# A decoder layer's opening: the conditioning vector spread by split fp32r products, half of the first input row block loaded from a second queue, weight casts before row copies

## The chip, the cores and the metric

The kernel runs on one core of a Trainium2 chip. The metric is device time in microseconds (us), from the first to the last work of the program on that core. The kernel before has a median of 720.72 us over 3 runs (719.94 to 721.26).

## The reference, cut to what matters

One layer of a decoder trunk, for 1024 tokens of 1024 channels, in float32:

```python
c_act = jax.nn.silu(c)
mod = c_act @ mod_w + mod_b                       # 1024 -> 3 x 1024
shift, scale, gate = jnp.split(mod, 3, axis=-1)
h = rmsnorm(x, norm_g) * (1.0 + scale) + shift
u = h @ w_in                                      # 1024 -> 5120
cv, cg, cs, lx, ls = split(u)
v = layernorm(causal_depthwise_conv(cv * sigmoid(cg), dw_w, dw_b))     # 31 taps
y_conv = (silu(v) @ pw2_w + pw2_b) * silu(cs)
xs = causal_depthwise_conv(lx, sc_w, sc_b)                              # 4 taps
r, i = sigmoid(xs @ wr + br), sigmoid(xs @ wi + bi)                     # block diagonal
hs = linear_scan(a(r), b(r, i, xs))
y_lru = hs * silu(ls)
x = x + (1.0 + gate) * (concat(y_conv, y_lru) @ w_out)
return rmsnorm(x, final_g)
```

## The kernel before

Channels lie on the 128 partitions, tokens along the free axis, so `x` is eight tiles `x0` to `x7` of 128x1024, and `T` = 1024, `H` = 512, `KT` = 8. Every large product is made in fp32r with the operands split in two: for an activation `u` and a weight `w`, `hi` is the value rounded to fp32r, `lo` the remainder, and three products `hi*hi`, `lo*hi`, `hi*lo` of 512 columns are added up in PSUM. ScalarE writes `hi` (a cast, a copy or a scaled activation), VectorE, GpSimd or an accumulating DMA makes `lo`.

All work is handed to a planner, class `Plan`. `S.op(engine, cost, emit, prio, reads, writes, ...)` records one step. `Plan.order` then plays the kernel forward with the costs written down and lets each engine take, of the steps that are ready, the one with the smallest priority; `Plan.run` emits the instructions in the order found. The order on each engine is therefore fixed when the kernel is built, and every engine works strictly through its own list. A table, `TURNS`, keyed by engine, first and last buffer of a step and a count, adds small amounts to priorities. `SP` stands for the queue from which nearly all loads are issued; loads accumulating in DRAM or SBUF are issued from GpSimd (`POOL`), stores of the last stage partly from ScalarE (`ACT`).

The opening, which sets when the first product of `w_in` can begin:

- `V` is a small table of all vectors, `c` among them, loaded first (L1483). SP's next loads are in the order of `LOADS`: `s0` (the first block of the transposed modulation matrix that gives `scale`, called `modw`), `w0` (weights of the first four output tiles for channel block 0, called `fraw`), `a0` and `b0` (the two halves of `x0`, 256 KB each), then `s1 w1 x1 s2 W2 x2` and so on.
- ScalarE makes `cs = silu(c)` as a 128x8 tile (L1834). `spread_c` (L1843) turns it into a row that lies on all partitions, `c_row`: for each of the 8 channel blocks a matmul whose stationary operand is one column of `cs`, repeated 128 times, and whose moving operand is the identity, in plain fp32. One such fp32 matmul is two instructions in the trace. Four blocks go into each of two PSUM tiles, `z` = 0 and 1.
- `first_dot` (L1938) multiplies `modw` by `c_row` on VectorE straight out of PSUM, in two halves, each with a sum along the row (L1434), and ScalarE copies `c_row` to SBUF as `sc`, at priority -101. The later blocks (`dot`, L1929) read `sc`. From the sums comes `gs`, one number per channel (L1961).
- `uh0`, the scaled `x0` rounded, comes from VectorE for the first half (L1456). `fhi` and `flo` are the split of `fraw`, `ul` the remainder of `uh`. `fw_mm` (L1884) then multiplies: 21 matmuls of 512 columns for each of the 8 channel blocks into the tiles called `first`.
- To keep TensorE at work meanwhile, 12 matmuls of a 128x128 tile of ones by itself, `idle_mm` (L1841, two instructions each, written into `token_stats`), stand in its list: 4 before the spread, 8 behind it (`IDLE`, `IDLE0`).

```python
cs, ps_c = ctile("cs", KT), [mm_tile(f"c_row{z}") for z in (0, 1)]
ACT(-130, lambda: cs, lambda: V[:, OFF["c"]:OFF["c"] + KT], AF.Silu, KT, w=[("cs", 0)])
def spread_c(z):
    for k in range(4 * z, 4 * z + 4):
        pe.matmul(half(ps_c[z], 0)()[:, k % 4 * P:k % 4 * P + P], cs[:, k:k + 1].to_broadcast([P, P]), ident,
                  start=True, stop=True)
```

After the opening come, in the order of the string `ORDER`, the other tiles of `u`: `iN` is output tile N of `w_in` (L1575, matmuls into `ps`), `gN` the two gate products of recurrence head N (`gates`, L2315, which read `xsh` and `xsl`, the split of `xs`), `iM+iN` two tiles done together with fewer products (`duo`, into `up` and `dn`; VectorE and GpSimd make the sums). Then come the recurrent half of `w_out` (`lru_pair`, `lx`, `lw`, `lc`; `lru_sums` makes the sums of activations it needs at a priority that holds `LTP`), `pw2`, and the other half of `w_out` with the last norm.

Of the kernel before, what the change touches and what calls it, by code (L numbers as in the profile page):

```python
# [9 lines left out]
F32 = mybir.dt.float32  # L10
F32R = mybir.dt.float32r
# [23 lines left out]
ORDER = "i10 i24 i2 g0 i25 i11 i3 i26 i33 i12 i4 g1 i34 i23 g2 i13 i35 i5 i27 g3 i20 i39 i14 i6 i28+i36 i15 i30+i37 i7 i29+i38 g6 g4 g5 i31 i19 i22+i18 g7 i21"  # L35
# [65 lines left out]
DENG = {14: ("POOL", "DMA", "DVE"), 17: ("POOL", "DVE", "DVE"), 20: ("DVE", "DVE", "DMA"), 21: ("DMA", "DMA", "DVE"), 24: ("DMA", "DVE", "POOL"), 26: ("DVE", "DMA", "DMA"), 27: ("POOL", "DMA", "POOL"), 30: ("DVE", "DVE", "DVE"), 35: ("DMA", "POOL", "DVE"), 36: ("POOL", "POOL", "POOL"), 39: ("DVE", "DVE", "POOL"), 40: ("DVE", "DVE", "DMA")}  # L101
# [7 lines left out]
LTP = 0.0  # L109
# [68 lines left out]
PDIRECT = (4,)  # L178
# [25 lines left out]
    ("ACT", "c1", "cq1_13", 0): -2.2,  # L204
# [39 lines left out]
    ("ACT", "cr4", "cr4", 0): 7.9,  # L244
    ("ACT", "cr4", "vha2", 0): 6.4,
# [43 lines left out]
    ("ACT", "r7", "r7", 0): -1.2,  # L289
    ("ACT", "r7", "r7", 1): -3.2,  # L290
# [73 lines left out]
    ("ACT", "vt1", "vhc1", 0): -0.1,  # L364
# [4 lines left out]
    ("ACT", "whi32", "wlo32", 0): -0.1,  # L369
    ("ACT", "whipw20", "wlopw20", 0): -2,  # L370
# [35 lines left out]
    ("DVE", "acc0", "lp0", 1): -0.3,  # L406
# [13 lines left out]
    ("DVE", "c2", "caccs2", 11): -0.1,  # L420
# [15 lines left out]
    ("DVE", "c4", "caccs4", 13): -0.2,  # L436
# [21 lines left out]
    ("DVE", "c6", "cacc6", 0): -0.6,  # L458
    ("DVE", "c6", "caccs6", 2): 1,
    ("DVE", "c6", "caccs6", 4): -0.5,  # L460
    ("DVE", "c6", "caccs6", 6): 2,
    ("DVE", "c6", "caccs6", 7): 0.2,
    ("DVE", "c6", "caccs6", 8): -0.3,
    ("DVE", "c6", "caccs6", 9): 1.6,
    ("DVE", "c6", "caccs6", 10): -2.4,
    ("DVE", "c6", "caccs6", 11): 1.5,
    ("DVE", "c6", "caccs6", 13): 1.4,
    ("DVE", "c6", "caccs6", 14): 2.6,
    ("DVE", "c6", "lnwide", 0): -0.3,
    ("DVE", "c6", "mean", 0): 0.3,  # L470
    ("DVE", "c6", "vla3", 0): -0.1,
    ("DVE", "c6", "vu3", 0): 2.7,
# [15 lines left out]
    ("DVE", "c7", "caccs7", 15): -0.1,  # L488
# [5 lines left out]
    ("DVE", "c7", "vt3", 1): -0.5,  # L494
    ("DVE", "cr0", "lnwide", 0): 3,
# [3 lines left out]
    ("DVE", "cr1", "vt0", 0): -1,  # L499
# [4 lines left out]
    ("DVE", "cr4", "mean", 0): 1.4,  # L504
    ("DVE", "csum", "c7", 0): -1,
# [4 lines left out]
    ("DVE", "fin0", "zout_0", 0): -2.7,  # L510
    ("DVE", "fraw0", "flo0", 0): 0.1,
# [28 lines left out]
    ("DVE", "rawout0_0", "rawout0_1", 1): -2,  # L540
# [9 lines left out]
    ("DVE", "rawpw21_1", "rawpw21_0", 0): -4,  # L550
# [6 lines left out]
    ("DVE", "sls3", "r3", 0): -0.1,  # L557
# [6 lines left out]
    ("DVE", "up33", "xs5", 0): -1,  # L564
    ("DVE", "up33", "xs5", 2): -0.2,
# [4 lines left out]
    ("DVE", "v0", "cacc0", 12): -0.3,  # L570
    ("DVE", "v0", "caccs0", 0): -0.2,
# [13 lines left out]
    ("DVE", "v2", "caccs2", 8): 0.2,  # L585
# [785 lines left out]
def hymba_layer(ctx: ExitStack, tc: tile.TileContext, xT, vecs, mod_w, w_first, w_in,  # L1371
# [229 lines left out]
    def half(b, i):  # L1601
        return part(b, i * H, i * H + H)
# [237 lines left out]
    def idle_mm():  # L1840
        pe.matmul(psb()[:, :P], ones, ones, start=True, stop=True)  # L1841
# [1244 lines left out]
```

## Time and profile before

| | |
|---|---|
| median of the runs | 720.72 us |
| profiled execution, its own time | 722.46 us |
| span of its instructions | 720.6 us |
| TensorE busy | 710.4 us (99%), 3230 matmuls |
| VectorE busy | 641.5 us (89%) |
| ScalarE busy | 477.3 us (66%) |
| GpSimd busy | 218.2 us (30%) |
| mean granted TensorE clock | 0.997 |

The page divides the span into busy time by engine; a matmul's record lasts until its result is written, so records of neighbouring matmuls overlap, and the time from one start to the next is what a matmul costs in a stream. The chain of work that ended last is followed back from the last instruction, at each step to what released it. A load is shown as the instruction that issues it and with the time from that issue to its landing.

### The profile page before, as it was taken

The numbers are of one execution on the slowest core, as the hardware profiler recorded it, in microseconds if no ns is written. First come the engines' busy times: TensorE is split into PE (matmuls) and PEld (weight loads), VectorE is DVE, ScalarE is ACT, GpSimd is POOL, SyncE is SP. The second block draws the span as 40 slices with busy tenths as digits, with TensorE's granted clock in tenths as the row PEclk, the third lists the DMA queues.
The fourth block names the chain that finished last, engine by engine and source line by source line (L and its number), as shares of the span: only waits on it lengthen the run. The fifth ranks groups of instructions, "written<-read, shape, count | busy, mean of one in ns | idle before, by whom it ended". The sixth has DMA issues, their size and how long they took to land.

```text
span 720.6 us, 9035 instructions
## 1 busy us (share of the span) xinstructions
PE 710.4 (99%) x3230; PEld 590.3 (82%) x3230; DVE 641.5 (89%) x885; ACT 477.3 (66%) x604; POOL 218.2 (30%) x188
## 2 busy tenths in 40 slices
PE   9999999999999999999999999999999999999995
PEld 8888888888888888888888888887887888878885
DVE  7989999799999989969988998998589976998747
ACT  7651598847857874974794979937589653744422
POOL 0022434543676752474162351100102100100001
PEclk9999999999999999999999999999999999999998
DMA  9935458999697999699664339999638755892006
GB/s 341 407 154 176 73 149 204 246 270 204 119 253 187 250 240 229 169 230 206 211 176 117 88 98 282 264 301 246 161 81 204 183 124 123 239 279 93 27 1 233
DMA packets 45500, 137.53 MB, mean 191 GB/s; under 512 B 5144, under 2 KB 14624, under 8 KB 45344
## 3 DMA queue, kind: packets, MB, share of 16 engines
q0 software_dynamic: 16848, 45.52, 35.2%
q1 hardware_dynamic: 27600, 90.53, 35.1%
q10 hardware_dynamic: 1008, 0.92, 0.4%
q8 instruction: 25, 0.41, 0.2%
q14 instruction: 19, 0.16, 0.1%
HBM read 84.22 MB, written 25.69 MB: 153 GB/s over the span
## 4 chain that ended last, share of the span: by engine, by line
PE 78%; DVE 10%; ACT 4%; issue 4%; DMA 3%; POOL 1%; DVEq 0%; POOLq 0%; ACTq 0%
PE ps L1575 34%; PE xpw L1751 6%; PE xout L1751 6%; PE first L1884 5%; PE dn L2713 3%; PE ypw L1751 3%; PE gate L2315 3%; PE dn L1575 3%; DVE caccs L1434 2%; PE up L1575 2%; PE lx L2468 2%; PE y L1721 1%; DMA wlo<-in_w_out_dram 1%; DMA wloout<-in_w_out_dram 1%; PE zpw L1751 1%
## 5 line engine op out<-in xcount | busy, mean ns | idle before, releaser
L1575 PE MATMUL ps<-uh,whi 128*128 128x512 f32 x448 | 138.0, 389 | 0.0
L1575 PE MATMUL ps<-uh,wlo 128*128 128x512 f32 x448 | 137.9, 389 | 0.0
L1575 PE MATMUL ps<-ul,whi 128*128 128x512 f32 x448 | 137.9, 389 | 0.0
L1575 PEld LDWEIGHTS ps<-uh,wlo 128*128 128x128 f32 x448 | 84.1, 188 | 17.5
L1575 PEld LDWEIGHTS ps<-ul,whi 128*128 128x128 f32 x448 | 84.1, 188 | 17.4
L1575 PEld LDWEIGHTS ps<-uh,whi 128*128 128x128 f32 x448 | 84.0, 188 | 17.4
L1434 DVE SCALAR_TENSOR_TENSOR cacc<-v,V,cacc 128x511 f32<-128x511 f32 (+14 forms) x90 | 66.5, 739 | 0.3
L1434 DVE SCALAR_TENSOR_TENSOR caccs<-v,V,caccs 128x511 f32<-128x511 f32 (+6 forms) x84 | 62.4, 743 | 1.0
L1434 DVE SCALAR_TENSOR_TENSOR caccs<-c,wsum,caccs 128x511 f32<-128x511 f32 (+6 forms) x84 | 62.2, 740 | 0.8
L1415 ACT CAST whi<-raw 128x1024 fp32r<-128x1024 f32 (+1 forms) x44 | 44.1, 1006 | 26.7 <-issue 14.0
L1423 ACT ACT_TABLE_LOAD x46 | 59.0, 1283 | 3.2 <-DVE r L2327 1.1
L1442 POOL TENSOR_TENSOR wlo<-raw,whi 128x1024 fp32r<-128x1024 f32 (+1 forms) x15 | 36.4, 2428 | 75.5 <-ACT whi L1415 73.5
L1447 POOL DMA_DIRECT2D es<-cq x30 | 28.3, 943 | 32.1 <-DMA es<-cq 11.1
L1434 DVE SCALAR_TENSOR_TENSOR modw<-modw,sc 128x1024 f32<-128x1024 f32 x23 | 32.7, 1425 | 0.0
L1442 DVE TENSOR_TENSOR wlo<-raw,whi 128x1024 fp32r<-128x1024 f32 (+1 forms) x22 | 30.7, 1395 | 0.6 <-ACT whi L1415 0.6
L1447 POOL DMA_DIRECT2D oo<-co x26 | 26.5, 1054 | 11.1 <-issue 5.5
L1423 ACT ACTIVATE uh<-x,shift 128x512 fp32r<-128x512 f32 x16 | 10.5, 713 | 23.9 <-PE ps L1575 23.9
L1442 POOL TENSOR_TENSOR o<-fin,bc 128x256 f32<-128x256 f32 (+1 forms) x6 | 4.9, 831 | 70.8 <-ACT bc L1415 70.8
L1447 POOL DMA_DIRECT2D accd<-acc x8 | 7.3, 914 | 62.1 <-ACT acc L1423 44.2
L1423 ACT ACTIVATE finsq<-fin 128x512 f32<-128x512 f32 (+2 forms) x14 | 7.9, 570 | 27.0 <-DVE fin L1434 15.1
L1423 ACT ACTIVATE cq<-v,V 128x511 f32<-128x511 f32 (+14 forms) x30 | 21.0, 707 | 6.5 <-DVE r L2327 3.1
L1447 POOL DMA_DIRECT2D lz<-in_w_out_dram x16 | 14.4, 987 | 34.4 <-ACT lz L1423 30.5
(525 smaller groups left out, 1937.8 us busy)
## 6 DMA issues: line engine op xcount, KB each, us to landing
raw<-in_w_in_dram SPq DMA_DIRECT2D x36, 512.0 KB, 4.6
modw<-in_mod_w_dram SPq DMA_DIRECT2D x24, 512.0 KB, 7.6
scsd<-scs SPq DMA_DIRECT2D x8, 512.0 KB, 3.9
raw<-in_w_out_dram SPq DMA_DIRECT2D x8, 512.0 KB, 4.5
accd<-acc POOLq DMA_DIRECT2D x8, 512.0 KB, 8.0
rawpw<-in_pw_dram SPq DMA_DIRECT2D x8, 512.0 KB, 3.9
scsr<-scsd SPq DMA_DIRECT2D x8, 512.0 KB, 4.3
rawout<-in_w_out_dram SPq DMA_DIRECT2D x8, 512.0 KB, 4.4
```

The costliest lines, as they stand in the source:

```text
L1415: act.copy(out(), in_())
L1423: act.activation(out=out(), in_=in_(), func=func, **kw)
L1434: dve.scalar_tensor_tensor(out=out(), in0=in0(), scalar=scalar, in1=in1(), op0=op0, op1=op1, accum_out=accum)
L1442: lambda: e.tensor_tensor(out=out(), in0=a(), in1=b(), op=op), prio, r, w,
L1447: return S.op("POOL", ISSUE, lambda: pool.dma_start(out(), a(), accum_op=ALU.add), prio, r, w, lag=RATE * n / T, after=after, flight=flight)
L1575: pe.matmul(ps()[:, a - off:b - off], k3(lhs)()[:, at, :], rhs[k]()[:, a:b], start=(k == first and lhs is wh and rhs is xh and (a - off) % ...
L1721: pe.matmul(to(), half(*lhs)()[:, j * P:j * P + P], half(*rhs)()[:, c0:c1], start=a == "S1" and j == 0 and t == 0, stop=j == KT // 2 - 1 a ...
L1751: pe.matmul(half(ps, 0)(), half(*lhs)()[:, j * P:j * P + P], half(*rhs)(), start=start and at == 0 and i == 0, stop=at == len(order) - 1 a ...
L1884: pe.matmul(ps()[:, a - off:b - off], fw_part(lhs, k, i * P, i * P + P)(), rhs()[:, a:b], start=k == 0 and lhs is wh and rhs is xh, stop=k ...
L2315: pe.matmul(ps()[:, c0:c1], lhs()[:, j, :], rhs()[:, c0:c1], start=st == 0, stop=st == 2)
L2468: pe.matmul(half(ps, h)(), lhs()[:, o:o + P], half(*rhs)(), start=begin and at == 0 and t == 0, stop=at == len(order) - 1 and t == len(ter ...
L2713: pe.matmul(half(ps, h)(), lhs()[:, o:o + P], half(rhs, z)(), start=begin and j == 0 and t == 0, stop=j == NJ - 1 and t == 2, skip_group_c ...
```

## The change

`silu(c)` is computed twice on ScalarE, once rounded to fp32r (`cs_hi`) and once in fp32 (`cs`); VectorE makes the remainder `cs_lo`. Instead of 8 fp32 matmuls by the identity, 16 fp32r matmuls are made, 8 with `cs_hi` and 8 with `cs_lo`, adding up in the same PSUM tiles. The identity is written as fp32r and read as fp32 elsewhere. The idle matmuls read one column of ones, repeated on both sides, instead of a 128x128 tile. The first half of `x0` is issued from ScalarE's queue as ScalarE's first step; SP no longer issues it. The copies of `c_row` to `sc` get priority -98.9 instead of -101, which is behind the cast of the first weights (-99). Beyond the opening, the gates of heads 4, 5, 6 and the pair of tiles 18 and 22 change their order in `ORDER`, `LTP` becomes -0.5, and some 135 lines of `TURNS` are added, removed or altered, nearly all in steps far behind the opening.

```diff
-ORDER = "... i29+i38 g6 g4 g5 i31 i19 i22+i18 g7 i21"
+ORDER = "... i29+i38 g4 g5 g6 i31 i19 i18+i22 g7 i21"
...
-DENG = {14: ("POOL", "DMA", "DVE"), ...}
+DENG = {14: ("POOL", "DMA", "DVE"), ..., 34: ("DVE", "DVE", "DVE"), ...}
...
-LTP = 0.0
+LTP = -0.5
...
-XADDP = -1.5
+XADDP = 0.3
 TSRC = "POOL"
 HSP = -60
+CSR, XQ, SCP = True, "ACT", -98.9
...
-CENG = {..., 22: "POOL", ...}
+CENG = {..., 22: "DVE", ..., 37: "POOL", 40: "DVE"}
...
-PDIRECT = (4,)
+PDIRECT = ()
...
-    ("ACT", "cr4", "cr4", 0): 7.9,
-    ("ACT", "cr4", "vha2", 0): 6.4,
+    ("ACT", "cr4", "cr4", 0): 7.6,
+    ("ACT", "cr4", "lnsq4", 0): -0.3,
+    ("ACT", "cr4", "vha2", 0): 6.1,
...
-    ident = const.tile([P, P], F32, tag="ident", name="ident")
-    make_identity(nc, ident)
+    ident_r = const.tile([P, P], F32R, tag="ident", name="ident")
+    ident = ident_r.bitcast(F32)
+    pool.memset(ident, 0.0)
+    pool.affine_select(out=ident_r, in_=ident, compare_op=ALU.not_equal, fill=1.0, base=0,
+                       pattern=[[-1, P]], channel_multiplier=1)
+    one = const.tile([P, 1], F32, tag="one", name="one")
+    dve.memset(one, 1.0)
...
-    ACT(-130, lambda: cs, lambda: V[:, OFF["c"]:OFF["c"] + KT], AF.Silu, KT, w=[("cs", 0)])
+    c_in = lambda: V[:, OFF["c"]:OFF["c"] + KT]
+    if CSR:
+        cs_hi, cs_lo = (const.tile([P, KT], F32R, tag=n, name=n) for n in ("cs_hi", "cs_lo"))
+        ACT(-130.2, lambda: cs_hi, c_in, AF.Silu, KT, w=[("cs", 1)])
+    ACT(-130, lambda: cs, c_in, AF.Silu, KT, w=[("cs", 0)])
+    if CSR:
+        S.op("DVE", 0.2, lambda: dve.tensor_tensor(out=cs_lo, in0=cs, in1=cs_hi.bitcast(F32), op=ALU.subtract),
+             -130, [("cs", 0), ("cs", 1)], [("cs", 2)], lock=True)
...
     def idle_mm():
-        pe.matmul(psb()[:, :P], ones, ones, start=True, stop=True)
+        pe.matmul(psb()[:, :P], one.to_broadcast([P, P]), one.to_broadcast([P, P]), start=True, stop=True)
+
+    def spread_part(z, part):
+        for k in range(4 * z, 4 * z + 4):
+            pe.matmul(half(ps_c[z], 0)()[:, k % 4 * P:k % 4 * P + P], part[:, k:k + 1].to_broadcast([P, P]),
+                      ident_r, start=part is cs_hi and k % 4 == 0, stop=part is cs_lo, skip_group_check=True)
...
             for z in (0, 1):
+                if CSR:
+                    for n, t in ((1, cs_hi), (2, cs_lo)):
+                        spread_op = S.op("PE", 0.055 * KT, lambda z=z, t=t: spread_part(z, t), -130, [("cs", n)],
+                                         [ps_c[z]], columns=P * KT // 2)
+                    continue
...
+        elif z == 0 and XQ == "ACT":
+            S.op("ACT", 0.05, lambda: act.dma_start(half(t, z)(), xT[:P // 2, :].rearrange(
+                "r (h f) -> (r h) f", h=2)), -140, [], halves(t, 0, H), moved=0.73)
...
-            ACT(-101, half(sc, z), half(ps_c[z], 0), "copy", H, r=[ps_c[z]], w=[(sc, z)],
+            ACT(SCP, half(sc, z), half(ps_c[z], 0), "copy", H, r=[ps_c[z]], w=[(sc, z)],
```

## Rows read from the trace of the kernel before

**Rows 1.** The page: busy time of the engines, share, instructions.
```profile
PE 710.4 (99%) x3230; PEld 590.3 (82%) x3230; DVE 641.5 (89%) x885; ACT 477.3 (66%) x604; POOL 218.2 (30%) x188
```

**Rows 2.** Windows, stages behind the opening: start:end, length, busy time by engine, clock.
```profile
60.00:270.00 210.00, 210.00 (x936) 174.12 (x935) 200.96 (x276) 151.80 (x193) 108.71 (x87) 1.00 0.82 200
270.00:460.00 190.00, 189.93 (x838) 156.97 (x837) 176.27 (x216) 143.30 (x159) 73.03 (x59) 1.00 0.72 185
460.00:510.00 50.00, 49.08 (x215) 39.99 (x215) 47.37 (x55) 31.95 (x39) 6.14 (x7) 1.00 0.92 256
510.00:560.00 50.00, 49.76 (x228) 40.69 (x227) 39.10 (x48) 38.51 (x50) 7.06 (x8) 1.00 0.63 150
560.00:650.00 90.00, 89.38 (x393) 73.36 (x392) 77.84 (x113) 51.08 (x68) 9.61 (x11) 1.00 0.70 187
```

**Rows 3.** The chain of work that ended last, 0 to 60 us: start, duration, what.
```profile
8.67 32.68 PE first L1884 x144
```

**Rows 4.** Timeline of TensorE, 0 to 14 us: start, duration, instructions merged.
```profile
1.06 2.07 PE L1841 MATMUL token_stats<-ones 128*128 128x128 f32 x8 [1.06 <-DVE ones L1492]
3.02 3.75 PE L1845 MATMUL c_row<-ident,cs 128*128 128x128 f32 x16
6.56 2.11 PE L1841 MATMUL token_stats<-ones 128*128 128x128 f32 x16
8.43 1.17 PE L1884 MATMUL first<-uh,fhi 128*128 128x512 f32 x4
...
13.31 0.84 PE L1884 MATMUL first<-uh,fhi 128*128 128x512 f32 x3
```

**Rows 5.** Timeline of VectorE, 5 to 9 us.
```profile
5.10 0.69 DVE L1434 SCALAR_TENSOR_TENSOR modw<-modw,c_row 128x512 f32<-128x512 f32 x1 [2.19 <-PE c_row L1845]
...
5.83 0.16 DVE L1948 TENSOR_TENSOR b<-a,b 128x1 f32<-128x1 f32 x1
6.81 0.69 DVE L1434 SCALAR_TENSOR_TENSOR modw<-modw,c_row 128x512 f32<-128x512 f32 x1 [0.82 <-PE c_row L1845]
...
7.79 0.49 DVE L1456 TENSOR_SCALAR uh<-x,gs 128x512 fp32r<-128x512 f32 x1
```

**Rows 6.** Timeline of ScalarE, 0 to 13 us.
```profile
0.74 1.28 ACT L1423 ACT_TABLE_LOAD   x1 [0.74 <-PEq L3078]
2.67 0.21 ACT L1423 ACTIVATE cs<-V 128x8 f32<-128x8 f32 x1 [0.64 <-DMA V<-in_vecs_dram]
...
6.38 0.62 ACT L1415 CAST fhi<-fraw 128x512 fp32r<-128x512 f32 x1
...
11.52 1.34 ACT L1423 ACTIVATE uh<-x,gs 128x512 fp32r<-128x512 f32 x2 [1.18 <-DVE gs L1961]
```

**Rows 7.** Timeline of SP's queue, 0 to 3 us: start and duration of an issue.
```profile
0.75 0.39 SPq L1483 DMA_DIRECT2D V<-in_vecs_dram  x1
1.20 0.42 SPq L1461 DMA_DIRECT2D modw<-in_mod_w_dram  x1
...
2.13 0.91 SPq L1461 DMA_DIRECT2D x<-in_xT_dram  x2
```

**Rows 8.** DMA issues between 1.1 and 1.3 us: size, us from issue to landing.
```profile
modw<-in_mod_w_dram SPq DMA_DIRECT2D x1, 512.0 KB, 3.6
V<-in_vecs_dram SPq DMA_DIRECT2D x1, 72.0 KB, 1.9
```

**Rows 9.** Windows of the opening; the last two columns are DMA share and GB/s.
```profile
2.00:3.00 1.00, 1.00 (x6) 0.85 (x5) 0.25 (x2) 0.34 (x4) 0.00 (x0) 1.00 1.00 329
3.00:4.00 1.00, 1.00 (x5) 1.00 (x5) 0.00 (x0) 1.00 (x1) 0.00 (x0) 1.00 0.88 234
...
9.00:10.00 1.00, 1.00 (x6) 0.83 (x5) 1.00 (x2) 0.98 (x2) 0.00 (x0) 1.00 1.05 424
```

**Rows 10.** Timelines of VectorE and TensorE about the gate of a head, 410 to 416 us.
```profile
411.23 1.29 DVE L1442 TENSOR_TENSOR xsl<-xs,xsh 128x1024 fp32r<-128x1024 f32 x1 [0.39 <-ACT xsh L1415]
...
412.68 0.62 PE L2315 MATMUL gate<-xsh,ghi 128*128 128x512 f32 x2
```

More of the change, by code (lines that the diff above doesn't have):

```diff
@@ L34 @@
 NEXT = (("in", LS), ("in", CS), ("in", CS + 1))
-ORDER = "i10 i24 i2 g0 i25 i11 i3 i26 i33 i12 i4 g1 i34 i23 g2 i13 i35 i5 i27 g3 i20 i39 i14 i6 i28+i36 i15 i30+i37 i7 i29+i38 g6 g4 g5 i31 i19 i22+i18 g7 i21"
+ORDER = "i10 i24 i2 g0 i25 i11 i3 i26 i33 i12 i4 g1 i34 i23 g2 i13 i35 i5 i27 g3 i20 i39 i14 i6 i28+i36 i15 i30+i37 i7 i29+i38 g4 g5 g6 i31 i19 i18+i22 g7 i21"
 EW = FW + len(NEXT) * P
@@ L100 @@
 WSUB = ("POOL", "POOL", "POOL")
-DENG = {14: ("POOL", "DMA", "DVE"), 17: ("POOL", "DVE", "DVE"), 20: ("DVE", "DVE", "DMA"), 21: ("DMA", "DMA", "DVE"), 24: ("DMA", "DVE", "POOL"), 26: ("DVE", "DMA", "DMA"), 27: ("POOL", "DMA", "POOL"), 30: ("DVE", "DVE", "DVE"), 35: ("DMA", "POOL", "DVE"), 36: ("POOL", "POOL", "POOL"), 39: ("DVE", "DVE", "POOL"), 40: ("DVE", "DVE", "DMA")}
+DENG = {14: ("POOL", "DMA", "DVE"), 17: ("POOL", "DVE", "DVE"), 20: ("DVE", "DVE", "DMA"), 21: ("DMA", "DMA", "DVE"), 24: ("DMA", "DVE", "POOL"), 26: ("DVE", "DMA", "DMA"), 27: ("POOL", "DMA", "POOL"), 30: ("DVE", "DVE", "DVE"), 34: ("DVE", "DVE", "DVE"), 35: ("DMA", "POOL", "DVE"), 36: ("POOL", "POOL", "POOL"), 39: ("DVE", "DVE", "POOL"), 40: ("DVE", "DVE", "DMA")}
 YDMA = (1, 3, 4, 6, 7)
@@ L128 @@
 TLO = ("POOL",) * 4
-CENG = {21: "POOL", 17: "DVE", 36: "DVE", 33: "POOL", 22: "POOL", 15: "POOL", 16: "DVE", 27: "POOL", 20: "POOL", 31: "POOL", 34: "POOL", 24: "POOL", 29: "POOL", 38: "POOL", 39: "DVE", 32: "POOL"}
+CENG = {21: "POOL", 17: "DVE", 36: "DVE", 33: "POOL", 22: "DVE", 15: "POOL", 16: "DVE", 27: "POOL", 20: "POOL", 31: "POOL", 34: "POOL", 24: "POOL", 29: "POOL", 38: "POOL", 39: "DVE", 32: "POOL", 37: "POOL", 40: "DVE"}
 LEV = ()
@@ L288 @@
     ("ACT", "r7", "a7", 0): -0.9,
[L289 to L290 removed]
+    ("ACT", "r7", "r7", 0): 0.8,
+    ("ACT", "r7", "r7", 1): 4.8,
     ("ACT", "raw21", "whi21", 0): 0.1,
@@ L383 @@
     ("ACT", "x7", "uh7", 1): 0.3,
+    ("ACT", "xpw2_0", "yc0", 0): 0.3,
     ("ACT", "xpw2_1", "yc2", 1): -0.3,
+    ("ACT", "xs2", "xsh2", 0): 2,
     ("ACT", "xs4", "xsh4", 0): 0.1,
@@ L457 @@
     ("DVE", "c5", "vu2", 0): 8.9,
[L458 to L470, printed above, removed]
+    ("DVE", "c6", "cacc6", 0): -0.3,
+    ("DVE", "c6", "caccs6", 0): 0.3,
+    ("DVE", "c6", "caccs6", 1): 0.3,
+    ("DVE", "c6", "caccs6", 2): 1.3,
+    ("DVE", "c6", "caccs6", 3): 0.3,
+    ("DVE", "c6", "caccs6", 4): -0.2,
+    ("DVE", "c6", "caccs6", 5): 0.3,
+    ("DVE", "c6", "caccs6", 6): 2.3,
+    ("DVE", "c6", "caccs6", 7): 0.5,
+    ("DVE", "c6", "caccs6", 9): 1.9,
+    ("DVE", "c6", "caccs6", 10): -2.1,
+    ("DVE", "c6", "caccs6", 11): 1.8,
+    ("DVE", "c6", "caccs6", 12): 0.3,
+    ("DVE", "c6", "caccs6", 13): 1.7,
+    ("DVE", "c6", "caccs6", 14): 2.9,
+    ("DVE", "c6", "caccs6", 15): 0.3,
+    ("DVE", "c6", "caccs6", 16): 0.3,
+    ("DVE", "c6", "mean", 0): 0.6,
     ("DVE", "c6", "vla3", 0): -0.1,
-    ("DVE", "c6", "vu3", 0): 2.7,
+    ("DVE", "c6", "vu3", 0): 3,
     ("DVE", "c7", "cacc7", 0): -2.4,
@@ L523 @@
     ("DVE", "modw22", "sc", 0): -0.2,
-    ("DVE", "ps16", "v4", 0): -1,
+    ("DVE", "ps16", "v4", 0): 1,
     ("DVE", "ps22", "xs3", 0): 3.7,
     ("DVE", "ps22", "xs3", 1): 4.1,
+    ("DVE", "ps35", "xs7", 0): -2,
+    ("DVE", "ps35", "xs7", 1): -2,
+    ("DVE", "ps35", "xs7", 2): -2,
     ("DVE", "ps4", "next4", 0): -0.2,
@@ L563 @@
     ("DVE", "up30", "xs6", 2): -2,
-    ("DVE", "up33", "xs5", 0): -1,
-    ("DVE", "up33", "xs5", 2): -0.2,
+    ("DVE", "up33", "xs5", 0): -0.7,
+    ("DVE", "up33", "xs5", 1): 0.3,
+    ("DVE", "up33", "xs5", 2): 0.1,
     ("DVE", "v0", "cacc0", 1): -0.1,
```

83 lines of the change are left out of this document (33 added, 50 removed).

## The prediction

> **What bounds the kernel now.** I read the page first: TensorE is busy 99% of the span, VectorE 89% [rows 1]. So only two things can move the end: when TensorE's stream of products starts, and the few places behind that where it waits. The chain of work has 144 products of 512 columns in 32.68 us without a break from 8.67 us on [rows 3], which is 0.227 us each. The stages say the same for the rest: no idle TensorE from 60 to 270 us, 0.07 us from 270 to 460, and then 0.92, 0.24 and 0.62 us in the three stages up to 650 us [rows 2], together 1.85 us. VectorE is busy 201 of 210 us and 176 of 190 us in the two long stages, so it is close behind.
>
> Then the opening, engine by engine. TensorE first: the first product starts at 8.43 us, and all before it is idle matmuls and the spread [rows 4]. The reader is to see two speeds in these rows. Eight idle matmul records take 1.06 to 3.02 us, 0.245 us each; 16 of the spread 3.02 to 6.56 us, 0.221 us each; and 16 idle ones of the same line as the first eight 6.56 to 8.43 us, 0.117 us each. The same instruction at half the time is TensorE at 1.2 GHz and then at 2.4 GHz, though the column of the granted clock says 1.00 throughout [rows 9]; I go by the records. The rise came at about 6.6 us, after 5.5 us of unbroken matmuls.
>
> VectorE's chain beside it: it waits 2.19 us for the first half of the spread, starts the first row sum at 5.10 us, waits another 0.82 us for the second half, starts the second sum at 6.81 us, and the scaled input `uh0` begins at 7.79 and ends at 8.28 us [rows 5]. So the product could have begun 1.62 us after the second sum's start. Both lines, the idle matmuls on TensorE and this chain, meet at 8.43 us within about 0.1 us: an earlier start needs both.
>
> **The change, part by part.**
>
> *The spread.* 16 fp32 records become 16 fp32r records. No row shows an fp32r matmul of 128 columns at the lower clock. From below: the 512-column fp32r product costs 0.227 us at the upper clock [rows 3], so 128 columns are 0.057 us, and 0.113 us at the lower. From above: 0.221 us, the record of now, if the weight load and not the columns sets the pace. I take 0.113, because the row of the same type has the load hidden. The spread then needs 16 x 0.113 = 1.8 us instead of 3.54 us, 1.73 us less.
>
> *What VectorE gains.* Now eight records end 2.08 us after the spread's start (3.02 to 5.10), of which 8 x 0.221 = 1.77 are the records and 0.31 the way out. After: first half ready at 3.02 + 0.90 + 0.31 = 4.23 us, second at 5.14 us. The first sum also needs `modw`, which lands 3.6 us after its issue at 1.20, at 4.80 us [rows 7, 8]. The half tile of `x0` is now in flight before it: 256 KB, at the 424 GB/s of a full stretch [rows 9] 0.62 us of all DMA engines. Bounds for what `modw` loses: 0, if these bytes fit into the stretch where DMA is 0.88 busy at 234 GB/s and into the time before 2 us, and 0.62. I take the middle, 0.31: the first sum starts at 5.11 us, as before. The second follows it by 0.73 + 0.16 us (the small addition ends at 5.99) instead of at 6.81 us. That is 0.81 us earlier, and the product could start at 7.62 us.
>
> *What TensorE gains.* The 1.73 us saved are at the lower clock. The 16 idle records behind the spread move up into that time and run at 0.221 us there; 1.73 / 0.221 = 8 of them are through before the time at which the clock rose, and each of these no longer costs 0.117 us behind it. That is 0.9 us: TensorE is free at 7.5 us. Had there been no idle matmuls, all 1.73 would come back; as it is, half does. The later of the two, 7.62 us, counts: the first product starts 0.8 us earlier. With `modw` on time it is 0.9 (TensorE's side), with `modw` late by the full 0.62 it is 0.5.
>
> *The first half of `x0` on ScalarE's queue.* It removes one issue from SP (half of the 0.91 us for both halves [rows 7]), so every load behind it, `b0` and `s1` first, is issued 0.45 us earlier. On ScalarE the issue, 0.4 us by SP's rows, stands before the table load of 1.28 us that starts at 0.74; ScalarE then waits 0.64 us for `V` [rows 6], which covers it. If the cover were gone, the whole opening would be late by what exceeds 0.64. `V` lands at 0.75 + 1.9 = 2.65 us [rows 7, 8] and now shares the engines with these 256 KB; bounds 0 and 0.62 us, I take 0.1, since `V` is 72 KB and issued in the same instant. That delays the spread, not `modw`, and stays within the 0.9 us by which the spread's first half is ahead.
> The Trainium skill (Trainium Kernel Development and Optimization, Key Constraints) says that loads issued from several queues run on the same 16 DMA engines, interleave, and save only issue time. By that rule the 0.62 us would fall on `modw` in full and the saving be 0.5 us instead of 0.8; the DMA share of 0.88 [rows 9] neither bears it out nor rules it out.
>
> *Second silu, subtraction, casts, constants.* The second silu is 0.21 us on ScalarE, of which 0.11 lies beside the first; the subtraction of 128x8 is some 0.2 us on VectorE. VectorE is idle 2.19 us there [rows 5], and the four matmuls with `cs_hi` last 0.45 us, so both cost nothing; without the cover 0.2 us. The cast `fhi` starts at 6.38 and takes 0.62 [rows 6]; a product at 7.62 needs it by then, and `flo` 0.9 us later. Putting the `sc` copies behind the cast frees it from waiting for the first sum, and VectorE reaches the first sum that reads `sc` only behind `uh0`, after 8.28 us [rows 5]. Nothing. The single column of ones lets the idle matmuls begin 0.1 us earlier, at a time when nothing waits. Nothing.
>
> *Does the gain stay?* One channel block is 21 products, 4.77 us; the second starts at 13.31 us [rows 4], and its input `uh1` comes from 11.52 to 12.86 us in two halves [rows 6], the first at 12.2. The product may move up 0.8 us and still find it, and VectorE's and the loads' part of it move up too. From there on TensorE does not wait, so 0.8 us is carried to 460 us, and past the waits there, as their causes hang on earlier products.
>
> *The rest of the diff.* Without effect, by the code: `PDIRECT` (tile 4 is not in `POOLED`), `XADDP` (`XADD` is False), entries 22 and 40 of `CENG` and 34 of `DENG` (pairs start at 27, 30, 33, 37), and 37 in `CENG`, which names the default. `LTP`, the two swaps in `ORDER` and `TURNS` only reorder steps with the same work. They can win at most the 1.85 us of waits [rows 2] and can lose as much or more; no row says which, and I take 0.
>
> **Sum.** The profiled execution took 722.46 us, 1.74 more than the median and 1.86 more than its span; less 0.8 it is 721.66. Against the median: 720.72 - 0.8 = 719.9 us.
>
> **Rivals.**
> - *The reordering removes waits.* Of 1.85 us some 0.7 to 1.85 goes as well: 718.1 to 719.2 us. For it: nearly all of them lie in 460 to 650 us, where `LTP` and most turns act. Against it: the 0.92 us stage has VectorE busy 47.4 of 50 us, and nothing takes work off it.
> - *The load of `x0` holds up `V` and `modw`.* Both by 0.62 us: spread from 3.64 us, TensorE free at about 7.8, the second sum at 6.3 and the product at 7.9, so 0.5 us is left: 720.2 us. It eats all the gain only where `modw` is 1.1 us late.
> - *The spread does not get faster*, if weight loads set the pace: 0.221 us again, 720.7 us. For it: no row prices a load of 128 columns alone. Against it: the 0.227 us of 512 columns.
> - *Slower: a split comes late for its gate.* The gate at 412.68 us has its `xsl` ready at 412.52 us [rows 10]; the margin is 0.16 us. If the new order puts VectorE steps of 1.28 us ahead of it, TensorE waits: two steps give 2.56 - 0.16 = 2.4 us, less the 0.8, 722.3 us. It is slower than before from 0.96 us of lateness, one step.
>
> **How the numbers follow.** Chances: as summed, 0.50 (own range 719.2 to 720.4); the reordering removes waits 0.27; loads in the way 0.08; spread not faster 0.06; late split 0.09. What a measurement of this kernel can tell from no change is 0.2%, 1.44 us, so faster means below 719.28. That is the second case but for its edge, 0.25, and the lower end of the first, 0.08: 0.33. Slower is the late split with two steps or more, 0.08. The rest, 0.59, is no difference. The range leaves out the best tenth of the second case and the worst of the late split: 718.2 to 721.3 us.
>
> **What would show it.** Right: `c_row` records 0.11 us apart, the second row sum at about 6.0 us, the first product at about 7.6 us, VectorE's first sum still waiting for `modw` and not for the spread, and the same 0.227 us stream behind it. Wrong: `c_row` at 0.22 us, `V` landing after 3 us, the first product still behind a queue of idle matmuls at 1.2 GHz, a second block that waits for `uh1`, or TensorE waits behind 400 us that rows 2 do not have.

## The result, and the profile after

The changed kernel has a median of 725.81 us over 16 runs, the kernel before 722.20 us over 16 runs beside it. The ratio is 1.0048 with a 95% interval of 1.0030 to 1.0065: by the medians 3.6 us slower. The prediction, 719.9 us in a range of 718.2 to 721.3 with a chance of 0.08 for slower, was wrong. The profiled execution took 724.15 us, against 722.46 us before. Times are medians: two executions of the experiments below lie far out (895.75 us in e2, 894.30 us in e3), and leaving them out would move those medians by 0.14 us at most.

The page of the changed kernel, against [rows 1], has 1.6 us more of TensorE, for the same 3230 matmuls:

```profile
PE 712.0 (99%) x3230; PEld 592.2 (82%) x3230; DVE 644.2 (89%) x887; ACT 477.1 (66%) x605; POOL 218.0 (30%) x188
```

The windows behind the opening, against [rows 2]:

```profile
60.00:270.00 210.00, 210.00 (x935) 174.12 (x935) 203.40 (x280) 149.99 (x191) 106.94 (x86) 1.00 0.80 201
270.00:460.00 190.00, 190.00 (x840) 157.29 (x839) 176.72 (x216) 142.38 (x159) 74.81 (x63) 1.00 0.72 183
460.00:510.00 50.00, 49.36 (x217) 40.17 (x216) 47.41 (x57) 32.32 (x39) 5.67 (x7) 1.00 0.92 262
510.00:560.00 50.00, 50.00 (x230) 41.25 (x229) 39.41 (x48) 38.98 (x52) 7.71 (x9) 1.00 0.65 157
560.00:650.00 90.00, 89.23 (x393) 73.12 (x392) 77.57 (x112) 50.70 (x69) 9.82 (x12) 1.00 0.71 189
```

TensorE's idle time there is 0.64 + 0.77 = 1.41 us, where it was 1.85. So in this execution TensorE lost nothing between 60 and 650 us; the loss must lie in the opening. Its timeline on TensorE, against [rows 4]:

```profile
0.93 2.08 PE L1849 MATMUL token_stats<-one 128*128 128x128 f32 x8 [0.93 <-DVE one L1491]
4.00 1.08 PE L1853 MATMUL c_row<-ident,cs_hi 128*128 128x128 f32 x4 [0.99 <-ACT cs L1419]
4.88 1.05 PE L1853 MATMUL c_row<-ident,cs_lo 128*128 128x128 f32 x4
5.73 1.05 PE L1853 MATMUL c_row<-ident,cs_hi 128*128 128x128 f32 x4
6.58 1.05 PE L1853 MATMUL c_row<-ident,cs_lo 128*128 128x128 f32 x4
7.44 3.72 PE L1849 MATMUL token_stats<-one 128*128 128x128 f32 x16
10.81 1.70 PE L1905 MATMUL first<-uh,fhi 128*128 128x512 f32 x4
12.34 1.09 PE L1905 MATMUL first<-uh,flo 128*128 128x512 f32 x4
13.27 1.07 PE L1905 MATMUL first<-ul,fhi 128*128 128x512 f32 x4
14.18 0.39 PE L1905 MATMUL first<-uh,fhi 128*128 128x512 f32 x1
```

Read it from one start to the next, as [rows 4] were read. Four terms add up to the fifth product, which began at 9.44 us and now begins at 12.34 us, 2.90 us later:

- The spread starts at 4.00 instead of 3.02 us: +0.98. TensorE stands idle for 0.99 us before it, which it did not before.
- The 16 records of the spread take 7.44 - 4.00 = 3.44 us instead of 3.54: 0.215 us each. The fp32r spread is no faster: -0.10.
- The 16 idle records take 10.81 - 7.44 = 3.37 us instead of 1.87, 0.211 us each instead of 0.117: +1.50.
- The first four products take 1.53 us instead of 1.01: +0.52.

The last two are TensorE's clock. Single records go from 0.213 us to half of it at 6.9 us before; here the products change from 0.43 us to 0.227 us at 12.0 us, so the rise from 1.2 to 2.4 GHz came 5.1 us later.

Why the spread starts late is on ScalarE and in the loads. ScalarE's timeline, against [rows 6], then the issues from 0.7 to 1.3 us with KB and us to landing, against [rows 8]:

```profile
0.74 0.41 ACTq L1882 DMA_DIRECT2D x<-in_xT_dram  x1
1.18 1.28 ACT L1419 ACT_TABLE_LOAD   x1 [1.18 <-PEq L3099]
3.64 0.21 ACT L1419 ACTIVATE cs_hi<-V 128x8 fp32r<-128x8 f32 x1 [1.18 <-DMA V<-in_vecs_dram]
```

```profile
modw<-in_mod_w_dram SPq DMA_DIRECT2D x1, 512.0 KB, 3.9
x<-in_xT_dram ACTq DMA_DIRECT2D x1, 256.0 KB, 3.1
V<-in_vecs_dram SPq DMA_DIRECT2D x1, 72.0 KB, 2.9
```

`V` takes 2.9 us to land instead of 1.9, and `modw` 3.9 instead of 3.6. ScalarE waits 1.18 us for `V` behind its table load, so the table load, though issued 0.44 us later, is covered. The DMA windows (last two columns: share, GB/s), against [rows 9]:

```profile
2.00:3.00 1.00, 1.00 (x5) 0.71 (x4) 0.00 (x0) 0.47 (x1) 0.00 (x0) 1.00 0.53 166
3.00:4.00 1.00, 0.01 (x2) 0.03 (x1) 0.26 (x3) 0.36 (x3) 0.00 (x0) 1.00 1.09 431
```

From 2 to 3 us less is moved than before (166 instead of 329 GB/s), and in the next microsecond more. With 256 KB beside it the small table does not come first: it lands 0.98 us later, 0.25 us ahead of the 256 KB.

VectorE, against [rows 5]:

```profile
5.97 0.69 DVE L1430 SCALAR_TENSOR_TENSOR modw<-modw,c_row 128x512 f32<-128x512 f32 x1 [1.82 <-PE c_row L1853]
...
7.68 0.69 DVE L1430 SCALAR_TENSOR_TENSOR modw<-modw,c_row 128x512 f32<-128x512 f32 x1 [0.82 <-PE c_row L1853]
...
8.66 0.49 DVE L1452 TENSOR_SCALAR uh<-x,gs 128x512 fp32r<-128x512 f32 x1
```

Both sums wait for the spread and nothing else. `uh0` ends at 9.15 us, 0.87 later than before, but the product does not begin until the idle matmuls are through at 10.81. In the opening TensorE's own list is the limit.

### The profile page after: what moved, and what is told of

Its sections match the earlier page's. It is cut to its first block, busy times and chain, and to the rows that moved or that the text cites. A ratio compares the mean times of both kernels' runs of the same rounds, so it can differ in the third digit from the quotient of the medians.

```text
span 722.4 us, 9036 instructions
## 1 busy us (share of the span) xinstructions
PE 712.0 (99%) x3230; PEld 592.2 (82%) x3230; DVE 644.2 (89%) x887; ACT 477.1 (66%) x605; POOL 218.0 (30%) x188
## 3 DMA queue, kind: packets, MB, share of 16 engines
q10 hardware_dynamic: 1152, 1.18, 0.5%
## 4 chain that ended last, share of the span: by engine, by line
PE 90%; DMA 3%; issue 3%; DVE 3%; POOL 0%; ACT 0%; DVEq 0%; POOLq 0%
PE ps L1576 42%; PE xout L1752 6%; PE first L1905 5%; PE xpw L1752 5%; PE dn L2734 4%; PE up L1576 3%; PE gate L2336 3%; PE dn L1576 3%; PE ypw L1752 3%; PE lx L2489 2%; PE up L2734 2%; PE zpw L1752 2%; PE y L1722 1%; DMA wlo<-in_w_out_dram 1%; DMA wloout<-in_w_out_dram 1%
## 5 line engine op out<-in xcount | busy, mean ns | idle before, releaser
L1438 DVE TENSOR_TENSOR wlo<-raw,whi 128x1024 fp32r<-128x1024 f32 (+1 forms) x22 | 27.9, 1267 | 0.0
```

The source lines that it names most:

```text
L1438: lambda: e.tensor_tensor(out=out(), in0=a(), in1=b(), op=op), prio, r, w,
```

## The experiments

Three theories stood at the start. *Load*: the half of `x0` on ScalarE's queue delays `V`, and with it everything. *Pace*: an fp32r record of 128 columns goes at the pace of its weight load and not of its columns, 0.213 us at 1.2 GHz, so nothing is won by it. *Clock*: such records also hold back the clock's rise, and the idle matmuls and first products pay. The first four kernels separate the load, the spread and the reordering. In what follows "fifth product" is its start against 9.44 us before, and "rise" the time from which single records take half as long.

**e1: the load back on SP.**

```diff
-CSR, XQ, SCP = True, "ACT", -98.9
+CSR, XQ, SCP = True, "SP", -98.9
```

> The changed kernel with the first half of x0 issued from SP's queue again, second behind w0; all else and the order of every other engine as in the changed kernel. Theory A (the load on ScalarE's queue holds up V): V lands at about 2.65 us instead of 3.62, the spread starts at about 3.0 instead of 4.00, and 1 us comes back, or half of it if TensorE still runs at 1.2 GHz: 0.5 to 1 us faster than the changed kernel, still slower than before. Theory B (the fp32r records take as long as the fp32 ones, 0.21 us, and TensorE stays longer at 1.2 GHz behind them): records of the spread still at 0.21 us, the 16 idle records behind it still at 0.21 us, the first product at about 10 us. Theory C (the pause of 1.4 us in front of the spread keeps the clock down): no pause any more, the idle records behind the spread at 0.11 us as before, first product at 8.4 us, 2.9 us faster than the changed kernel.

725.46 us, ratio 1.0026 (1.0008 to 1.0045). Its TensorE timeline:

```profile
2.93 1.09 PE L1853 MATMUL c_row<-ident,cs_hi 128*128 128x128 f32 x4
...
6.37 3.72 PE L1849 MATMUL token_stats<-one 128*128 128x128 f32 x16
9.75 1.75 PE L1905 MATMUL first<-uh,fhi 128*128 128x512 f32 x4
11.33 1.09 PE L1905 MATMUL first<-uh,flo 128*128 128x512 f32 x4
```

The spread starts on time, without a pause ahead of it, and takes 3.44 us all the same. Its idle records stay at 0.211 us, the rise is at 11.0 us, the fifth product 1.89 us late. So the late `V` alone does not make the clock late.

**e2: the fp32 spread, the load still on ScalarE's queue.**

```diff
-CSR, XQ, SCP = True, "ACT", -98.9
+CSR, XQ, SCP = False, "ACT", -98.9
```

> The changed kernel with one silu and the spread by 8 fp32 matmuls (16 records) as before; the first half of x0 stays on ScalarE's queue. Theory A: V still lands at about 3.6 us and the spread starts at 4.0; TensorE's pause before it stays. Theory B: the clock rises earlier than at 11.96 us though the pause is there, the idle records behind the spread run partly at 0.11 us, and the first product starts between 8.9 and 9.6 us: 1.5 to 2 us faster than the changed kernel, 1 us slower than before. Theory C: the clock still rises at about 12 us, first product near 10.8 us, no faster than the changed kernel.

724.21 us, ratio 1.0005 (0.9989 to 1.0021). `V` lands 3.6 us after its issue, the spread starts at 4.72 us, the rise is at 9.7 us, the fifth product 2.23 us late.

```profile
4.72 3.76 PE L1858 MATMUL c_row<-ident,cs 128*128 128x128 f32 x16 [1.72 <-ACT sp_u L1419]
8.27 2.63 PE L1849 MATMUL token_stats<-one 128*128 128x128 f32 x16
```

**e3 and e4: both taken back.** e3 also restores the copies' priority and the full tile of ones, so that only the reordering behind the opening is left; e4 keeps those two small edits.

```diff
-CSR, XQ, SCP = True, "ACT", -98.9
+CSR, XQ, SCP = False, "SP", -101      # e3
+CSR, XQ, SCP = False, "SP", -98.9     # e4
```

> The changed kernel with the whole opening of before (fp32 spread, x0 from SP, copies of c_row at -101, idle matmuls of a 128x128 tile), so that only the reordering and the turns behind it are left of the change. Theory D (the reordering costs something): as slow as the changed kernel, 3 us above before. Against it (all is lost in the opening, and the reordering gives 1.1 us back, as the gap between the two traces shrinks from 2.9 us at 46 us to 1.8 us at the end): first product at about 8.4 us and 1.1 us faster than before.

> The changed kernel with the fp32 spread and x0 from SP's queue, but with the new place of the c_row copies and the idle matmuls that read one column of ones. If these two are free: the same time as with the whole old opening, within 0.2%. If the idle matmuls from one repeated column keep the clock down: records behind the spread at 0.21 us and a time 2 us above it.

e3 722.05 us, ratio 0.9980 (0.9965 to 0.9995); e4 722.04 us, 0.9976 (0.9957 to 0.9994). The two small edits cost and bring nothing. The rise is at 4.3 and 5.2 us, the fifth product 0.49 and 0.64 us early. All four share the runs of the kernel before (723.11 us); among them the load costs 724.21 - 722.04 = 2.2 us, the fp32r spread 725.46 - 722.04 = 3.4 us. The two do not add up: against e4's fifth product, e2's is 2.87 us late with the load alone, e1's 2.53 with the fp32r spread alone, and the changed kernel's, with both, 3.54 (2.77 to 3.54 in four profiles, p1 to p3 below among them).

**e5: the same fp32r spread, but 256 columns wide.** If the weight load sets the pace, columns of zeros beside the identity are free, and if the late rise goes with the narrow records, wider ones bring the early rise back. 12 of the 16 records get them, on top of e1. The tile of ones is left out as well; what read it reads the single column.

```diff
-    ident_r = const.tile([P, P], F32R, tag="ident", name="ident")
+    wide_r = const.tile([P, 2 * P], F32R, tag="ident", name="ident")   # zeros | identity
+    ident_r = wide_r[:, P:]
...
+            w = P * (k % 4 > 0)
-            pe.matmul(half(ps_c[z], 0)()[:, k % 4 * P:k % 4 * P + P], ..., ident_r, ...)
+            pe.matmul(half(ps_c[z], 0)()[:, k % 4 * P - w:k % 4 * P + P], ..., wide_r[:, P - w:], ...)
```

> The fp32r spread with x0 from SP's queue (as e1_x_on_sp), but in 12 of its 16 records the moving operand is 256 columns, the identity with 128 columns of zeros beside it, so that the same sums come out and TensorE has columns to do in the time that a record takes anyway. The only change in what is computed is that zeros are added. Theory B1 (an fp32r record of 128 columns takes 0.21 us because its weight load does, and TensorE, with columns in half of that time only, stays at 1.2 GHz for longer): the wide records take 0.21 us as well, the clock rises as early as with the fp32 spread (4 to 7 us in the traces so far, against 11 to 12 with fp32r), and the time is that of e4_x_sp_fp32, 3.4 us below e1_x_on_sp. Theory B2 (it is something else about the split spread: the type, the longer chain of silu, remainder and product): no faster than e1_x_on_sp, the clock still rises at about 11 us.

722.36 us, ratio 0.9986 (0.9969 to 1.0004; kernel before beside it 722.51 us), where e1 had 1.0026. Its TensorE timeline:

```profile
2.95 1.19 PE L1853 MATMUL c_row<-ident,cs_hi 128*128 128x128 f32 x4
3.94 1.05 PE L1853 MATMUL c_row<-ident,cs_lo 128*128 128x128 f32 x4
4.79 1.05 PE L1853 MATMUL c_row<-ident,cs_hi 128*128 128x128 f32 x4
5.64 0.98 PE L1853 MATMUL c_row<-ident,cs_lo 128*128 128x128 f32 x4
6.46 1.95 PE L1848 MATMUL token_stats<-one 128*128 128x128 f32 x16
8.28 1.17 PE L1905 MATMUL first<-uh,fhi 128*128 128x512 f32 x4
```

From 3.94 to 5.64 us a group of four takes 0.85 us, as in e1, although three of the four have twice the columns. So the columns do not set the pace of the narrow records. The weight loads (PEld) do keep it, four in 0.85 us, in e1 (first two lines) as in e5 (last two), which fits *Pace*:

```profile
3.71 0.97 PEld L1853 LDWEIGHTS c_row<-ident,cs_lo 128*128 128x128 f32 x4
4.56 0.97 PEld L1853 LDWEIGHTS c_row<-ident,cs_hi 128*128 128x128 f32 x4
```

```profile
3.73 0.97 PEld L1853 LDWEIGHTS c_row<-ident,cs_lo 128*128 128x128 f32 x4
4.58 0.97 PEld L1853 LDWEIGHTS c_row<-ident,cs_hi 128*128 128x128 f32 x4
```

How a load and its columns share the 0.213 us is not shown: 256 columns alone would need as much at this clock, by half of the 0.427 us that 512 take. The idle records behind the spread take 0.114 us, the rise is at 6.4 us, the fifth product 0.16 us early: *Clock* holds. The 4.6 us between the two rises are more than executions with the same opening differ by here (2.6 at most). The instructions and their number are those of e1, and the spread takes about as long (3.51 us against 3.44); the columns differ.

**e6: fewer idle matmuls behind the narrow spread** (e1 with `IDLE` 6 instead of 12).

> The fp32r spread with x0 from SP's queue (as e1_x_on_sp) and 2 idle matmuls behind the spread instead of 8. Theory B (the clock rises late, and behind the spread 16 idle records at 0.21 us stand in front of the first product): the first product starts when uh0 is ready, at about 8.3 us instead of 9.75, and runs at 1.2 GHz until the clock rises; up to 11 us some 6 products of 0.43 us are done where there were 3, so 0.7 us is won against e1_x_on_sp. If the clock comes still later without the idle matmuls: nothing is won or some is lost.

725.53 us, ratio 1.0038 (1.0017 to 1.0060): no gain. The product starts at 8.36 us instead of 9.75, but at the lower clock, 0.43 us each, until 13.5 us:

```profile
6.50 1.16 PE L1849 MATMUL token_stats<-one 128*128 128x128 f32 x4
8.36 2.04 PE L1905 MATMUL first<-uh,fhi 128*128 128x512 f32 x4 [0.69 <-DVE uh L1452]
10.20 1.91 PE L1905 MATMUL first<-uh,flo 128*128 128x512 f32 x4
11.91 1.84 PE L1905 MATMUL first<-ul,fhi 128*128 128x512 f32 x4
```

The thirteenth product starts at 13.58 us, where e1 has it at 13.17. In these two profiles the rise comes 2.5 us later with fewer idle matmuls and a wait of 0.69 us, and that takes back what the shorter queue gives.

**e7: the load on ScalarE's queue, but behind the silu** (e2 with the issue moved to 2.66 us).

> The changed kernel with the fp32 spread (as e2_fp32_spread), but the first half of x0 is issued from ScalarE's queue behind the silu instead of as ScalarE's first step, at about 2.9 us instead of 0.74. Theory A1 (x0's bytes are ahead of V's and modw's in the DMA engines): V lands at 2.65 us again and modw at 4.8, and the time is that of e4_x_sp_fp32, 2.1 us below e2_fp32_spread. Theory A2 (it is the second queue as such, or the issue on ScalarE, that costs): V at 2.65 us, but the opening as late as in e2_fp32_spread. x0's half lands later and could then be what uh0 waits for, beyond 7.3 us; that would show as uh0 starting later than 7.2 us with the sums done.

725.40 us, ratio 1.0021 (1.0003 to 1.0039). `V` lands on time again, the spread starts at 3.00 us, the rise is at 6.7 us, which bears out *Load*. But the half tile now lands 6.6 us after its issue, and `uh0` waits for it:

```profile
7.53 0.22 DVE L1985 SCALAR_TENSOR_TENSOR gs<-macc,b,V 128x1 f32<-128x1 f32 x1
9.37 0.49 DVE L1452 TENSOR_SCALAR uh<-x,gs 128x512 fp32r<-128x512 f32 x1 [1.62 <-DMA x<-in_xT_dram]
```

The fifth product is 1.57 us late.

**e8: fewer idle matmuls behind the fp32 spread** (e4 with `IDLE` 8).

> The fp32 spread with x0 from SP's queue (as e4_x_sp_fp32), the faster version so far, with 4 idle matmuls behind the spread instead of 8. If the idle records are what holds the first product when the clock rises late: up to 0.9 us less in those executions and nothing in the others, so 0 to 0.5 us below e4_x_sp_fp32 in the median. If the pause that opens in front of the first product keeps or brings the clock down: slower by up to 1 us.

721.97 us, ratio 0.9994 (0.9974 to 1.0014), on the chip of e5 to e7. The product waits 0.85 us for `uh` and starts at 8.01 us: no gain over e4.

**e9: the wide spread in the changed kernel itself**, with the load on ScalarE's queue (e5 with `XQ` "ACT").

> The changed kernel with 12 of the 16 records of the spread 256 columns wide (128 columns of zeros beside the identity), the first half of x0 still on ScalarE's queue. Theory clock (narrow fp32r records keep TensorE at 1.2 GHz): the idle records behind the spread go at 0.11 us at least in their later part, the first product starts near 9.5 us instead of 10.81, and the ratio falls from 1.0048 to about 1.001 to 1.0025, beside 1.0005 of the kernel with the fp32 spread and the same load. Theory late start (the clock rises late because V comes late and TensorE pauses before the spread, not because of the record's width): the idle records stay at 0.213 us, the first product at 10.8 us, ratio 1.004 to 1.006.

723.55 us, ratio 1.0030 (1.0014 to 1.0047): between the two theories, and so neither alone.

```profile
4.03 1.19 PE L1853 MATMUL c_row<-ident,cs_hi 128*128 128x128 f32 x4 [1.03 <-ACT cs L1419]
...
7.58 3.22 PE L1848 MATMUL token_stats<-one 128*128 128x128 f32 x16
10.56 1.17 PE L1905 MATMUL first<-uh,fhi 128*128 128x512 f32 x4
```

TensorE pauses 1.03 us for the late `V`, and the rise comes at 10.2 us instead of the 6.4 of the same spread without the pause (e5); the fifth product is 2.13 us late. e2 has 9.7 us with the pause and e4 5.2 without, both with the fp32 spread. So the late `V` costs twice: its own microsecond, and a later clock behind TensorE's pause. In the changed kernel either cause is enough for a late rise: narrow records without the pause have 11.0 us (e1), the pause without narrow records 10.2 and 9.7 (e9, e2). What the width of the records adds behind such a pause is small beside the scatter: p1 below, with narrow ones, has 10.2 us as well.

**e10: e4 once more on another chip.**

> The kernel of the fourth run (fp32 spread, both halves of x0 on SP, the rest of the change kept) once more on the chip of this call. If the reordering behind the opening is worth what the first comparison showed, the ratio to the kernel before is 0.996 to 0.9995 again; if that comparison was favoured by its runs of the kernel before, it lies between 0.9995 and 1.001, as that of the same kernel with four idle records fewer did (0.9994).

721.38 us, ratio 0.9992 (0.9976 to 1.0008). Here e4 is not separated from the kernel before. Its profile repeats e4's opening: rise at 5.6 us, fifth product 0.55 us early.

**p1 to p4: where the median's other 1.9 us are.** The medians differ by 3.6 us, the first two profiles by 1.7. Three more profiled executions of the changed kernel and one of e4:

> The changed kernel, one more profiled execution. Theory waits: if its time is over 726 us, TensorE is busy 187 to 188 of the 190 us from 270 to 460 us and waits on VectorE there, and the first product starts near 10.8 us as in the first profile; if it is under 725.5 us, 189.5 to 190. Theory opening: an execution over 726 us has its first product, or the change to 0.23 us per product, 2 us later than the first profile, and 190 of 190 us.

> As the run before it: over 726 us with 187 to 188 of 190 us and the first product near 10.8 us by theory waits; with a later opening and 190 of 190 us by theory opening.

> As the two runs before it. Of three executions one or two should be over 726 us, as 8 of 16 were.

> The fourth kernel (fp32 spread, both halves of x0 on SP), one more profiled execution. 1 of its 12 times was over 725 us. Theory waits: 720 to 722.5 us and TensorE busy 189 to 190 of 190 us from 270 to 460 us; in the rare execution over 724 us the same 2.3 to 2.6 us of waits. Theory opening: a time over 723 us goes with a change to 0.11 us per idle record later than 6.9 us.

| execution | time, us | fifth product, us late | rise, us | TensorE idle 60 to 650, us |
|---|---|---|---|---|
| before [rows 2, 4] | 722.46 | 0 | 6.9 | 1.85 |
| changed, first | 724.15 | 2.90 | 12.0 | 1.41 |
| p1 | 725.12 | 2.13 | 10.2 | 2.61 |
| p2 | 724.39 | 2.39 | 10.8 | 1.56 |
| p3 | 726.29 | 2.81 | 11.7 | 2.27 |
| e4 | 720.88 | -0.64 | 5.2 | 1.37 |
| p4 (e4) | 722.63 | -0.56 | 5.6 | 2.50 |

Neither theory holds as worded: p3, the one over 726 us, opens no later than the first profile, and TensorE is busy 189.16 of the 190 us from 270 to 460 us. All four executions of the changed kernel open 2.1 to 2.9 us late. What differs between them is mostly waits behind the opening. Counted matmul by matmul against the first profile, p1 is 0.8 us ahead at 12 us and 1.0 us behind at the end, p2 0.5 ahead and 0.2 behind, p3 0.1 ahead and 2.1 behind. The steps lie at a gate at 232 us (p1, p3) and between 290 and 340 us (p2, p3). The column of idle time shows only a part of this (p3 2.27, the first 1.41). In p1, by the view of waits (us in total, times, longest):

```profile
PE gate L2336 <- ACT scs L1419: 1.4, 1, 1.4
...
PE zout L1752 <- DMA wloout<-in_w_out_dram: 0.8, 1, 0.8
```

None of the four executions of the changed kernel has the 2.3 to 2.6 us of idle TensorE between 270 and 460 us that the profiled executions of e5, e7 and e9 had. So the opening accounts for 2.1 to 2.9 us at the fifth product, against the one profile of the kernel before. The rest of the 3.6 us is not traced to a cause: waits behind the opening move single executions by 1 to 2 us, and whether the changed kernel has them more often than the one before is open.

## Why the prediction was wrong, step by step

**The failed step: "I take 0.113, because the row of the same type has the load hidden".** The record measured 0.215 us, the upper bound that I had written beside it (0.221). The row of 512 columns, at 0.227 us each, says nothing of 128: by e5, 128 columns go at the pace of 256. The spread was to be 1.73 us shorter and was 0.10 shorter. The rival "the spread does not get faster", at 0.06, was the right mechanism. Its price, 720.7 us, was not, because of what followed from it.

**The second half of the same failure: the rise of the clock "at about 6.6 us", held fixed.** The whole sum on TensorE's side let 8 idle records pass "before the time at which the clock rose" and never asked whether the new records would move that time. They do: 11.0 us in e1 against 6.4 in e5 with the same instructions at the same pace but wider. The late rise is worth 1.50 + 0.52 us in the first profile, the larger part of the 2.90; the late start less the shorter spread is the other 0.88. How much of it is the records' and how much the pause's can't be split there, as either brings a late rise alone. No rival had it. The reason given beside the rows, that the rise came "after 5.5 us of unbroken matmuls", took unbroken matmuls for enough, whatever their type and width, and one execution for a fixed time: e3, with the same opening, rose at 4.3 us.

**The load of `x0`: right rival, too small.** `V` was to lose 0.1 us with bounds of 0 and 0.62; it lost 0.98, and 1.7 in e2. The bound was the transfer time of the 256 KB alone. The statement that the delay "stays within the 0.9 us by which the spread's first half is ahead" fell with the spread. What made up the excess over 0.62 is not shown; `modw` lost 0.38, near the 0.31 taken. What the rival lacked is the pause of TensorE, which e9 shows to put off the clock as well. The rule of the Trainium skill (Trainium Kernel Development and Optimization, Key Constraints) that loads from several queues interleave on the same engines, cited against the change, pointed the right way: the trace agrees with it, `V` and `modw` being 0.98 and 0.38 us later, and SP's 0.45 us of issue time won nothing that TensorE saw.
On the pace, the Trainium skill (TensorE: Matmul & The Clock Gate, LDWEIGHTS) puts a weight load at columns / 1.2, which is 0.107 us for 128. The runs show twice that from one fp32r load to the next at the lower clock, 0.213 us, with 128 as with 256 columns, and for the price of a record this decides. It does not refute the page: 0.107 us for a load and 0.107 for 128 columns behind it, a quarter of the 0.427 us of 512, would be the same sum, and no run times a load by itself.

**Right.** Order of copies, the single column: nothing, as e3 and e4 agree. Second silu and subtraction: nothing, as in e1 the spread starts at 2.93 us and runs without a gap. The table load put off by the issue was covered (1.18 us of waiting for `V` behind it). The step "From there on TensorE does not wait, so 0.8 us is carried to 460 us" held for the loss in the first profile: no idle TensorE from 60 to 460 us.

**The reordering, taken as 0, did what its rival said, less strongly.** In the first profiles 2.90 us of loss at 12 us are 1.8 us at the end (spans of 722.4 and 720.6), and 0.44 of the 1.1 us given back are the windows' idle time. Matmul by matmul the rest is found: the changed kernel is 2.9 us late up to 330 us, 2.6 from 340, 2.4 from 500, 1.7 from 580 and 2.0 from 650 us on. The largest step, 0.7 us between 550 and 580 us, is as large in e3's profile, which is 0.7 us early at 550 and 1.4 at 580. The late split for a gate, the rival that would have made it slower, doesn't show: where p1 and p3 wait at a gate at 232 us, it is for ScalarE, by the view of waits. e3, which is the reordering alone, has 0.9980, and e10, with two small edits besides, 0.9992: between nothing and 0.4%.

**The signs named ahead.** Three of the marks of "wrong" came true at once: `c_row` at 0.22 us, `V` past 3 us, the first product behind idle matmuls at 1.2 GHz. The chain of work ([rows 3]) shows the stream itself unchanged:

```profile
11.16 33.10 PE first L1905 x144
```

144 products in 33.10 us, 0.4 more than before, and the first of them are those at the lower clock.

**The base.** The forecast of 719.9 us stands on a median of 3 runs, 720.72 us; beside the changed kernel the one before has 722.20 us over 16. Of the 5.9 us between forecast and result 1.5 are this, 0.8 the gain that did not come and 3.6 the loss.

**The best version** is e4, the change without the fp32r spread and with both halves of `x0` on SP: 722.04 us against 723.11 on one chip (0.9976), 721.38 against 722.01 on another (0.9992). Both ratios lie below the changed kernel's 1.0048 with intervals that do not touch, though that kernel was not timed beside them; against the kernel before only the first is clear of noise.

## What to carry to other kernels

Do not price a short matmul by its columns alone, and look for the row that has the shape in question: a row of the same type with four times the columns can hide the load and says nothing. Before filling or thinning TensorE's work ahead of a clock rise, ask what the edit does to the time of the rise; records as long as before, and as unbroken, can come with a later rise. And a transfer issued early on a second queue is paid by the small load that everything waits for: compare where each ends, not where each is issued.

## What the runs showed of the hardware that was not expected

The clock's rise by kernel, from single records, with what TensorE did before it:

| what stood ahead | kernels | rise, us |
|---|---|---|
| no pause, fp32 spread or 256 columns | before, e3, e4, e5, e7, e8, e10, p4 | 4.3 to 6.9 |
| pause of 1 us or more for `V`, fp32 spread or 256 columns | e2, e9 | 9.7, 10.2 |
| no pause, fp32r spread of 128 columns | e1 | 11.0 |
| the same, then a wait of 0.69 us for `uh` | e6 | 13.5 |
| pause of 1 us, fp32r spread of 128 columns | changed, p1, p2, p3 | 10.2 to 12.0 |

TensorE's records are back to back and its busy share is 1.00 through the spread in e1 as in e5, so neither the busy share nor the page's clock column (1.00 throughout the opening) shows the difference; only the spacing of equal records does. The trace's own record of the granted clock begins only at the rise, at 6.88 us before and 11.96 after, the times that the spacing gives. The fp32 records of 128 columns have the 0.213 us of the fp32r records and the early rise of those of 256 columns; why was not measured. Even with the same opening the rise moved by 1.8 us between executions (10.2 to 12.0 in four of the changed kernel), which alone is 0.8 us at the fifth product, and by 2.6 us between the kernel before and e3 (6.9 and 4.3).
